# Seven products for eight in half of the up projections, with the sums of weights on GpSimd

## The chip, the core and the metric

The kernel runs on one core of a Trainium2 chip. The metric is the device time of one execution in microseconds (us). Engines: PE (TensorE, matrix products), PEld (its weight loads), DVE (VectorE), ACT (ScalarE), POOL (GpSimd), SP (the queue that issues the weight loads). Each engine works through its own queue in order; semaphores hold an instruction until what it reads is there and what it overwrites is free.

## The reference, cut to what matters

One decoder layer on 256 tokens, width 2048, everything float32: a feed-forward, a token-mixing block, a second feed-forward, a layer norm behind each.

```python
def swiglu(x, w_up, w_down):                 # w_up [2048, 2 * 5632], w_down [5632, 2048]
    a, u = jnp.split(x @ w_up, 2, axis=-1)
    return (jax.nn.silu(a) * u) @ w_down

h = layer_norm(ALPHA * h + 0.5 * swiglu(h, w_ffn1_up, w_ffn1_down), ln1_g, ln1_b)
h = layer_norm(ALPHA * h + token_mix(h, ...), ln2_g, ln2_b)
h = layer_norm(ALPHA * h + 0.5 * swiglu(h, w_ffn2_up, w_ffn2_down), ln3_g, ln3_b)
```

## The kernel before, in words

**Precision.** PE multiplies in float32r, so that each float32 operand is split into a high and a low part, h + l (`split`): ACT copies and rounds the source to h (L92), DVE subtracts h from the source to get l (L93). A product is three matmuls: ah·wh, ah·wl, al·wh.

**A product of activations and weights** is `gemm`. Activations lie feature-major in pages of 128 x 1024 (four k tiles of 128 rows by 256 tokens). Weights come in groups of 512 rows by 512 columns, 1 MB each, which SP loads into one of three `raw` buffers; each group is split in two halves of 128 x 1024 into `wh` and `wl`, four buffers each. A half serves 12 matmuls (2 k tiles, 2 token tiles of 128, 3 matmuls). The two sums of 128 tokens by 512 columns are PSUM banks `acc`.

**The feed-forward** (`ffn`) goes over 11 chunks j of 512 hidden columns. Chunk j is two gemms of 4 groups over the same activations: columns j of the half a, and columns NFF + j of the half u, 192 matmuls together. Then ACT takes tanh and DVE makes silu(a) * u (L206 to L208) in `tmp`; PE transposes it in 8 transposes (L166), which are put behind a group of the next chunk (`later`, `tick`), and the result is split into the next pages. After all 11 chunks `project_norm` does the down projection in 4 gemms of 11 groups, adds the residual (L235) and does the layer norm; the reciprocal root in it is the only arithmetic of POOL (L245, one column).

**Order.** The kernel is written in a framework that puts the instructions into each engine's queue by priority and by its own costs; what stands in the queues is fixed when the program is built.

Of the kernel before, what the change touches and what calls it, by code (L numbers as in the profile page):

```python
# [36 lines left out]
GL0 = 10  # L37


class Layer:  # L40
# [58 lines left out]
    def raw(self, shape=(P, 4, 512)):  # L99
        return self.tile("raw", list(shape), F32, 3)  # L100

    def load_w(self, src, paged=False, cut=None):
# [4 lines left out]
        out = []
        for i in range(2):
            if cut is not None:
                cut(i)  # L110
                self.nc.sync.dma_start(raw[:, 2 * i:2 * i + 2, :], src[:, 2 * i:2 * i + 2, :])
            if paged:
                h, l = (self.page(F32R).rearrange("p (k n) -> p k n", k=2) for _ in range(2))
            else:
                h = self.tile("wh", [P, 2, 512], F32R, 4)
                l = self.tile("wl", [P, 2, 512], F32R, 4)
            self.split(h, l, raw[:, 2 * i:2 * i + 2, :])
            out.append((h, l))
# [69 lines left out]
    def ffn(self, xh, xl, w_up, w_down, resid, g, b, finish, before_last=None, before=None, cut=None,  # L188
# [3 lines left out]
        hh, hl = [], []  # L192

        def place(ts, ph, pl):
            for tt in range(2):
# [1 line left out]
            yield

        for j in range(NFF):
            a = self.gemm(act, w_up[j], 4, head=4 if j == 0 and before is None else 0, before=before if j == 0 else None,  # L200
                          cut=cut if j == 0 else None)
            u = self.gemm(act, w_up[NFF + j], 4)
            ph, pl = self.page(F32R), self.page(F32R)
            ts = [self.tmp(), self.tmp()]
            for tt, t in enumerate(ts):
                nc.scalar.activation(t, a[tt], AF.Tanh, scale=0.5)  # L206
                nc.vector.scalar_tensor_tensor(t, t, 1.0, a[tt], op0=ALU.add, op1=ALU.mult)  # L207
                nc.vector.scalar_tensor_tensor(t, t, 0.25, u[tt], op0=ALU.mult, op1=ALU.mult)  # L208
# [481 lines left out]
```

## Time and profile before

| | |
|---|---|
| median of three timed runs | 2240.55 us (2240.1 to 2241.12) |
| span of the profiled execution, from its first to its last instruction | 2238.4 us |
| PE, share of the span in which it is busy | 99% |
| DVE | 56% |
| ACT | 43% |
| POOL | 2% |
| granted TensorE clock, mean | 0.998 |
| mean transfer rate | 198 GB/s |

The three runs and the profiled span agree within 0.13%. The profile lists, for each engine, when each instruction ran, and what ended the idle time before it; the granted clock is the share of TensorE's full speed.

### The profile page before, as it was taken

The numbers are of one execution on the slowest core, as the hardware profiler recorded it, in microseconds if no ns is written. First come the engines' busy times: TensorE is split into PE (matmuls) and PEld (weight loads), VectorE is DVE, ScalarE is ACT, GpSimd is POOL, SyncE is SP. The second block draws the span as 40 slices with busy tenths as digits, with TensorE's granted clock in tenths as the row PEclk, the third lists the DMA queues.
The fourth block names the chain that finished last, engine by engine and source line by source line (L and its number), as shares of the span: only waits on it lengthen the run. The fifth ranks groups of instructions, "written<-read, shape, count | busy, mean of one in ns | idle before, by whom it ended". The sixth has DMA issues, their size and how long they took to land.

```text
span 2238.4 us, 24924 instructions
## 1 busy us (share of the span) xinstructions
PE 2215.9 (99%) x10056; PEld 1838.5 (82%) x10056; DVE 1248.9 (56%) x1404; ACT 958.2 (43%) x1075; POOL 51.2 (2%) x93
## 2 busy tenths in 40 slices
PE   8999999999999999999999999999999999999997
PEld 6888888888888888888888888878888888888886
DVE  5555555554455757675566556675555555454445
ACT  4444444443334444554444444444444444443332
POOL 0000000010000100000000000010000000000000
PEclk9999999999999999999999999999999999999999
DMA  7555555565556645455655556666555555565553
GB/s 261 191 188 188 188 188 188 189 253 205 199 188 228 233 170 182 169 184 188 207 179 194 199 193 220 235 221 239 188 188 188 189 190 191 188 211 197 188 192 128
DMA packets 65956, 442.34 MB, mean 198 GB/s; under 512 B 7905, under 2 KB 7905, under 8 KB 15537
## 3 DMA queue, kind: packets, MB, share of 16 engines
q1 hardware_dynamic: 57888, 414.21, 52.4%
q0 software_dynamic: 6656, 22.36, 3.4%
q10 hardware_dynamic: 1296, 4.19, 0.5%
q8 instruction: 78, 1.28, 0.2%
q14 instruction: 38, 0.30, 0.0%
HBM read 434.44 MB, written 6.29 MB: 197 GB/s over the span
## 4 chain that ended last, share of the span: by engine, by line
PE 96%; DVE 2%; DMA 1%; issue 0%; ACT 0%; POOL 0%; POOLq 0%; ACTq 0%; DVEq 0%
PE acc L133 93%; PE tr L166 2%; PE tr L282 1%; DMA pg<-in_xT 1%; DVE wl L93 0%; DVE pg L562 0%; DMA tmp<-in_w_pool 0%; DVE gt L252 0%; DVE m L561 0%; PE tr L314 0%; DVE pg L93 0%; DVE gt L254 0%; DVE stats L236 0%; DVE gt L235 0%; POOL mv L245 0%
## 5 line engine op out<-in xcount | busy, mean ns | idle before, releaser
L133 PE MATMUL acc<-wh,pg 128*128 128x512 f32 x5120 | 1594.2, 390 | 0.0
L93 DVE TENSOR_TENSOR wl<-raw,wh 128x1024 fp32r<-128x1024 f32 x772 | 944.4, 1224 | 917.2 <-ACT wh L92 916.7
L92 ACT CAST wh<-raw 128x1024 fp32r<-128x1024 f32 x772 | 812.7, 1054 | 1130.6 <-PE acc L133 1099.2
L133 PEld LDWEIGHTS acc<-wh,pg 128*128 128x128 f32 x5120 | 961.2, 188 | 198.3
L133 PE MATMUL acc<-wl,pg 128*128 128x512 f32 x2560 | 996.4, 389 | 0.0
L133 PEld LDWEIGHTS acc<-wl,pg 128*128 128x128 f32 x2560 | 480.7, 188 | 98.0
L133 PE MATMUL acc<-wh,gt 128*128 128x512 f32 x1056 | 332.8, 391 | 7.8 <-ACT wh L92 7.2
L133 PEld LDWEIGHTS acc<-wh,gt 128*128 128x128 f32 x1056 | 198.9, 189 | 49.3 <-ACT wh L92 7.2
L133 PE MATMUL acc<-wl,gt 128*128 128x512 f32 x528 | 206.4, 391 | 1.0 <-DVE wl L93 1.0
L133 PEld LDWEIGHTS acc<-wl,gt 128*128 128x128 f32 x528 | 99.6, 189 | 22.2 <-DVE wl L93 1.8
L92 ACT CAST pg<-tr 128x512 fp32r<-128x512 f32 x82 | 44.7, 586 | 20.4 <-PE tr L166 19.8
L93 DVE TENSOR_TENSOR pg<-tr,pg 128x512 fp32r<-128x512 f32 x82 | 52.5, 682 | 0.6 <-ACT pg L92 0.3
L206 ACT ACTIVATE tmp<-acc 128x512 f32<-128x512 f32 x44 | 26.2, 595 | 26.0 <-PE acc L133 26.0
L207 DVE SCALAR_TENSOR_TENSOR tmp<-tmp,acc 128x512 f32<-128x512 f32 x44 | 30.1, 684 | 10.3 <-ACT tmp L206 10.3
L133 PE MATMUL acc<-pg,pg 128*128 128x512 f32 x144 | 34.5, 392 | 0.8 <-DVE pg L93 0.7
L133 PEld LDWEIGHTS acc<-pg,pg 128*128 128x128 f32 x144 | 26.8, 188 | 7.1 <-DVE pg L93 1.6
L166 PEld LDWEIGHTS tr<-ident,tmp 128*128 128x128 f32 x240 | 27.9, 140 | 3.9
L166 PE MATMUL tr<-ident,tmp 128*128 128x128 f32 x240 | 31.0, 272 | 0.0
L208 DVE SCALAR_TENSOR_TENSOR tmp<-tmp,acc 128x512 f32<-128x512 f32 x44 | 28.1, 680 | 0.0
L235 DVE SCALAR_TENSOR_TENSOR gt<-gt,acc 128x512 f32<-128x512 f32 x24 | 15.7, 682 | 21.5 <-PE acc L133 21.5
L282 PE MATMUL tr<-pg,pg 128*128 128x256 f32 (+2 forms) x168 | 26.3, 302 | 0.0
L93 DVE TENSOR_TENSOR pg<-raw,pg 128x1024 fp32r<-128x1024 f32 x18 | 21.7, 1217 | 4.5 <-ACT pg L92 4.5
(99 smaller groups left out, 418.4 us busy)
## 6 DMA issues: line engine op xcount, KB each, us to landing
raw<-in_up SPq DMA_DIRECT2D x175, 1024.0 KB, 4.8
raw<-in_down SPq DMA_DIRECT2D x88, 1024.0 KB, 4.8
raw<-in_w_in SPq DMA_DIRECT2D x88, 1024.0 KB, 4.8
raw<-in_w_out SPq DMA_DIRECT2D x16, 1024.0 KB, 5.1
raw<-in_w_kv SPq DMA_DIRECT2D x8, 1024.0 KB, 5.0
raw<-in_br_att SPq DMA_DIRECT2D x8, 1024.0 KB, 4.8
h_d<-gt POOLq DMA_DIRECT2D x16, 256.0 KB, 3.6
raw<-in_br_pool SPq DMA_DIRECT2D x4, 1024.0 KB, 4.8
```

Source lines behind the costliest of these rows:

```text
L92: self.nc.scalar.copy(h, src)
L93: self.nc.vector.tensor_sub(l, src, h.bitcast(F32))
L133: nc.tensor.matmul(accs[tt], lhsT=a, rhs=b, start=kt == 0 and i == 0, stop=kt == kts - 1 and i == 2)
L166: self.nc.tensor.transpose(t[:, i * P:(i + 1) * P], src[:, i * P:(i + 1) * P], self.ident)
L206: nc.scalar.activation(t, a[tt], AF.Tanh, scale=0.5)
L207: nc.vector.scalar_tensor_tensor(t, t, 1.0, a[tt], op0=ALU.add, op1=ALU.mult)
L208: nc.vector.scalar_tensor_tensor(t, t, 0.25, u[tt], op0=ALU.mult, op1=ALU.mult)
L235: nc.vector.scalar_tensor_tensor(zz, zz, ALPHA, accs[tt], op0=ALU.mult, op1=ALU.add)
L282: self.nc.tensor.matmul(out, lhsT=a, rhs=b, start=start and i == 0, stop=stop and i == 2)
```

## The change

Both feed-forwards are changed; the token mixing keeps its order of work.

**Seven for eight.** In a chunk j > 0 the groups of k, 512 rows each, are treated jointly for both token tiles, both halves of k and both column blocks (a and u): a 2 x 2 by 2 x 2 block product, eight block products of 6 matmuls each. In two of the four groups (`SEVEN`) they are done in the Strassen-Winograd manner as seven: one is between sums of the activations (`forms`, made once for each feed-forward) and sums of weight quarters. The weight quarters b00, b10, b01, b11 are halves of 128 x 1024. Four sums of them are made by POOL in place: two (below called A and B) at the head of a group, C and D one after the other later. Each of the seven multiplies its own split operand, so that a group of seven splits 7 halves in place of 4, and each split half serves 6 matmuls. The other two groups stay at eight products, but take their token difference from `forms`. At the end of a chunk eight instructions combine seven PSUM banks to the four results.

**Columns in three parts.** The 11 chunks come as 4, 4 and 3 (`HIDDEN`); behind each part comes its share of the down projection, which is added to the residual in SBUF (`Norm.add`).

**Buffers.** `raw` is 9 halves in place of 3 whole groups, and every load is 512 KB in place of 1 MB; pages 23 in place of 27, `tmp` 6 in place of 4; PSUM is one pool of 8 banks in place of 4 and 4. x's pages come from the pool `pg`; memory pages are loaded in the first two groups of the last gemm of the first feed-forward.

```diff
+PAGES = dict(pg=23, gt=6)
+HIDDEN = ((0, 4), (4, 8), (8, NFF))
+SEVEN = (True, True, False, False)
...
-    def raw(self, shape=(P, 4, 512)):
-        return self.tile("raw", list(shape), F32, 3)
+    def raw(self, shape=(P, 2, 512)):
+        return self.tile("raw", list(shape), F32, 9)
+
+    def load_half(self, src, i):
+        raw = self.raw()
+        self.nc.sync.dma_start(raw, src[:, 2 * i:2 * i + 2, :])
+        return raw
...
+    def seven(self, act, forms, modes, w0, w1):
...
+        def product(g, bank, lhs, w, last):
...
+            for k in range(2):
+                ah, al = lhs(k)
+                for i, (a, b) in enumerate(((ah, w[0]), (ah, w[1]), (al, w[0]))):
+                    nc.tensor.matmul(banks[bank], lhsT=a, rhs=b[:, k, :], start=bank not in first,
+                                     stop=last and k == 1 and i == 2)
...
+        def singles(g, end):
+
+            b00, b10 = self.load_half(w0[g], 0), self.load_half(w0[g], 1)
+            b11 = self.load_half(w1[g], 1)
+            b01 = self.load_half(w1[g], 0)
+            s00 = self.halves(b00)
+            nc.gpsimd.tensor_add(b00, b00, b01)
+            nc.gpsimd.tensor_add(b01, b01, b11)
+            product(g, 1, quarter(g, 0, 0), s00, g == sevens[-1])
+            s10 = self.halves(b10)
+            product(g, 2, quarter(g, 0, 1), s10, end)
+            s11 = self.halves(b11)
+            product(g, 3, form(g, 3), s11, end)
+
+            def sums():
+                t1 = self.halves(b00)
+                nc.gpsimd.tensor_add(b00, b00, b11)
+                product(g, 5, form(g, 0), t1, end)
+                t2 = self.halves(b00)
+                nc.gpsimd.tensor_add(b00, b00, b10)
+                product(g, 6, form(g, 1), t2, g == sevens[-1])
+                t3 = self.halves(b01)
+                product(g, 7, form(g, 2), t3, g == sevens[-1])
+                t4 = self.halves(b00)
+                product(g, 4, quarter(g, 1, 1), t4, end)
+
+            return sums
...
+        for g in range(groups):
+            end = g == groups - 1
+            if modes[g]:
+                after = singles(g, end)
+            else:
+                eight(g, end)
+                after = None
+            if behind is not None:
+                behind()
+            behind = after
+            self.tick()
...
+        u, c00, v, c11 = (self.tmp() for _ in range(4))
+        nc.scalar.copy(u, banks[1])
+        nc.vector.tensor_add(c00, u, banks[2])
+        nc.vector.tensor_add(u, u, banks[6])
+        nc.vector.tensor_add(v, u, banks[7])
+        nc.vector.tensor_sub(u, banks[5], u)
+        nc.vector.tensor_sub(c11, banks[5], v)
+        nc.vector.tensor_add(u, u, banks[3])
+        nc.vector.tensor_add(v, v, banks[4])
+        return [[c00, u], [v, c11]]
```

The order of a chunk is thus: three single quarters of group 0, three of group 1, the four sums t1 to t4 of group 0, the four quarters of group 2 (eight products), t1 to t4 of group 1, the four quarters of group 3.

DVE's queue at the border of two chunks before: `tmp` is the chunk that ended, `wl` are halves of the next one.

```order
L93 TENSOR_TENSOR wl_1039<-raw_1036,wh_1038 128x1024
L208 SCALAR_TENSOR_TENSOR tmp_978<-tmp_978,acc_838 128x512
L208 SCALAR_TENSOR_TENSOR tmp_979<-tmp_979,acc_839 128x512
L93 TENSOR_TENSOR wl_1043<-raw_1036,wh_1042 128x1024
L93 TENSOR_TENSOR wl_1073<-raw_1070,wh_1072 128x1024
```

DVE's queue in the changed kernel, behind the last matmul of a chunk (the first row needs it): the end of that chunk, the three singles of the next chunk's group 1 (`wl_1198`, `wl_1210`, `wl_1220`).

```order
L287 TENSOR_TENSOR tmp_1117<-acc_883,tmp_1117 128x512
L288 TENSOR_TENSOR tmp_1120<-acc_883,tmp_1119 128x512
L289 TENSOR_TENSOR tmp_1117<-tmp_1117,acc_824 128x512
L290 TENSOR_TENSOR tmp_1119<-tmp_1119,acc_917 128x512
L352 SCALAR_TENSOR_TENSOR tmp_1131<-tmp_1131,tmp_1118 128x512
L96 TENSOR_TENSOR wl_1198<-raw_1189,wh_1197 128x1024
L353 SCALAR_TENSOR_TENSOR tmp_1131<-tmp_1131,tmp_1117 128x512
L352 SCALAR_TENSOR_TENSOR tmp_1132<-tmp_1132,tmp_1119 128x512
L96 TENSOR_TENSOR wl_1210<-raw_1191,wh_1209 128x1024
L353 SCALAR_TENSOR_TENSOR tmp_1132<-tmp_1132,tmp_1120 128x512
L96 TENSOR_TENSOR pg_1130<-tr_1182,pg_1129 128x4x128
L96 TENSOR_TENSOR wl_1220<-raw_1193,wh_1219 128x1024
```

Two instructions of the chunk that ended stood between two halves; now ten do (of its eight combinations four, the four of silu, a transposed split), and they stand among the splits of three halves.

The next rows of DVE's queue are t1, t2, t3, t4 of group 0 and the first quarter of group 2; with what each waits for.

```order
L96 TENSOR_TENSOR wl_1230<-raw_1139,wh_1229 128x1024 [waits Pool_49]
L96 TENSOR_TENSOR wl_1242<-raw_1139,wh_1241 128x1024 [waits PE_49,Activation_49]
L96 TENSOR_TENSOR wl_1254<-raw_1145,wh_1253 128x1024 [waits Activation_49]
L96 TENSOR_TENSOR wl_1265<-raw_1139,wh_1264 128x1024 [waits Activation_49]
L96 TENSOR_TENSOR wl_1291<-raw_1282,wh_1290 128x1024 [waits DMAHW5_49,Activation_49]
```

POOL's queue in that chunk: A and B of group 0 (`raw_1139` is its b00), A and B of group 1 (`raw_1189`), C and D of group 0, C and D of group 1.

```order
L231 TENSOR_TENSOR raw_1139<-raw_1139,raw_1145 128x1024 [waits DMAHW5_49,DMAHW0_49,DVE_49]
L232 TENSOR_TENSOR raw_1145<-raw_1145,raw_1143 128x1024 [waits DMAHW7_49,Pool_49]
L231 TENSOR_TENSOR raw_1189<-raw_1189,raw_1195 128x1024 [waits DMAHW1_49,DMAHW4_49,DVE_49,Activation_49]
L232 TENSOR_TENSOR raw_1195<-raw_1195,raw_1193 128x1024 [waits DMAHW6_49,DMAHW3_49,Pool_49]
L241 TENSOR_TENSOR raw_1139<-raw_1139,raw_1143 128x1024 [waits DVE_49,Activation_49]
L244 TENSOR_TENSOR raw_1139<-raw_1139,raw_1141 128x1024 [waits DMAHW6_49,DVE_49]
L241 TENSOR_TENSOR raw_1189<-raw_1189,raw_1193 128x1024 [waits DVE_49]
L244 TENSOR_TENSOR raw_1189<-raw_1189,raw_1191 128x1024 [waits DMAHW2_49,DVE_49]
```

Before, none of these eight stood there. C overwrites b00, which t1's split reads, so it stands behind that subtraction; t2's copy on ACT reads what C wrote; D overwrites b00 again behind t2's subtraction, and t4's copy reads what D wrote.

PE's queue there: the products of t2 (`wh_1241`), t3 (`wh_1253`) and t4 (`wh_1264`), then group 2 (`wh_1290`).

```order
L215 MATMUL acc_1246<-wh_1241,pg_252 128x512 [waits Activation_49]
L215 MATMUL acc_1257<-wh_1253,pg_252 128x512 [waits Activation_49]
L215 MATMUL acc_1246<-wl_1242,pg_252 128x512 [waits DVE_49]
...
L215 MATMUL acc_1268<-wh_1264,pg_71 128x512 [waits Activation_49]
...
L215 MATMUL acc_1164<-wh_1290,pg_73 128x512 [waits Activation_49]
L215 MATMUL acc_1268<-wl_1265,pg_71 128x512 [waits DVE_49]
```

Of the chunk's 188 PE instructions (180 matmuls and 8 transposes) 64 stand ahead of that last row, the 8 transposes among them, and 124 matmuls from it on.

## Rows read from the trace of the kernel before

**Rows 1.** The page: span, then busy us of each engine, its share, instructions.
```profile
span 2238.4 us, 24924 instructions
PE 2215.9 (99%) x10056; PEld 1838.5 (82%) x10056; DVE 1248.9 (56%) x1404; ACT 958.2 (43%) x1075; POOL 51.2 (2%) x93
```

**Rows 2.** Stretches: us, PE, PEld, DVE, ACT, POOL busy (x), PEclk, DMA share, GB/s.
```profile
40.00:515.00 475.00, 475.00 (x2142) 394.26 (x2141) 248.74 (x236) 201.92 (x213) 8.50 (x16) 1.00 0.56 197
560.00:765.00 205.00, 205.00 (x916) 169.90 (x915) 117.58 (x123) 86.20 (x86) 8.00 (x11) 1.00 0.60 211
1300.00:1510.00 210.00, 208.39 (x939) 171.43 (x939) 134.61 (x156) 88.06 (x95) 17.25 (x31) 1.00 0.62 218
```

**Rows 3.** Chain that ended last, in order of time: start us, us, what.
```profile
61.46 43.54 PE acc L133 x192
105.88 43.54 PE acc L133 x192
```

**Rows 4.** The page's groups: line engine op out<-in | busy, mean ns | idle before.
```profile
L93 DVE TENSOR_TENSOR wl<-raw,wh 128x1024 fp32r<-128x1024 f32 x772 | 944.4, 1224 | 917.2 <-ACT wh L92 916.7
L92 ACT CAST wh<-raw 128x1024 fp32r<-128x1024 f32 x772 | 812.7, 1054 | 1130.6 <-PE acc L133 1099.2
```

**Rows 5.** Timeline inside a chunk: start us, us, engine, line, [idle before <-releaser].
```profile
305.34 1.05 ACT L92 CAST wh<-raw 128x1024 fp32r<-128x1024 f32 x1 [1.67 <-PE acc L133]
...
306.43 1.22 DVE L93 TENSOR_TENSOR wl<-raw,wh 128x1024 fp32r<-128x1024 f32 x1 [1.49 <-ACT wh L92]
```

**Rows 6.** Timeline of DVE in a stretch without idle time.
```profile
1493.32 1.22 DVE L93 TENSOR_TENSOR pg<-raw,pg 128x1024 fp32r<-128x1024 f32 x1
1494.45 1.22 DVE L93 TENSOR_TENSOR wl<-raw,wh 128x1024 fp32r<-128x1024 f32 x1
1495.59 0.68 DVE L235 SCALAR_TENSOR_TENSOR gt<-gt,acc 128x512 f32<-128x512 f32 x1
1496.19 1.22 DVE L93 TENSOR_TENSOR pg<-raw,pg 128x1024 fp32r<-128x1024 f32 x1
```

**Rows 7.** POOL's arithmetic, all six: duration ns min/median/max.
```profile
L245 POOL TENSOR_TENSOR mv<-mv,mhalf x6: 922/932/2101, 736.2 to 2229.0; 128x1 f32<-128x1 f32 x6
```

**Rows 8.** Timelines of POOL and of DVE around the first of them.
```profile
736.18 0.93 POOL L245 TENSOR_TENSOR mv<-mv,mhalf 128x1 f32<-128x1 f32 x1 [238.52 <-DVE mv L244]
...
735.95 0.74 DVE L252 SCALAR_TENSOR_TENSOR gt<-gt,mv,gt 128x512 f32<-128x512 f32 x1
737.14 0.22 DVE L246 SCALAR_TENSOR_TENSOR mv<-mv 128x1 f32<-128x1 f32 x1 [0.46 <-POOL mv L245]
```

**Rows 9.** Timelines of POOL and of DVE around the longest of them.
```profile
752.23 2.10 POOL L245 TENSOR_TENSOR mv<-mv,mhalf 128x1 f32<-128x1 f32 x1
...
751.36 1.41 DVE L252 SCALAR_TENSOR_TENSOR gt<-gt,mv,gt 128x512 f32<-128x512 f32 x2
752.68 1.22 DVE L93 TENSOR_TENSOR wl<-raw,wh 128x1024 fp32r<-128x1024 f32 x1
754.37 0.22 DVE L246 SCALAR_TENSOR_TENSOR mv<-mv 128x1 f32<-128x1 f32 x1 [0.47 <-POOL mv L245]
```

**Rows 10.** The page's DMA issues: KB each, median us from issue to landing.
```profile
raw<-in_up SPq DMA_DIRECT2D x175, 1024.0 KB, 4.8
```

**Rows 11.** Timeline of DVE at the end: first and last of one token half's norm.
```profile
2216.07 0.69 DVE L235 SCALAR_TENSOR_TENSOR gt<-gt,acc 128x512 f32<-128x512 f32 x1 [8.57 <-PE acc L133]
...
2222.66 1.41 DVE L254 SCALAR_TENSOR_TENSOR gt<-gt,mv,pg 128x512 f32<-128x512 f32 x2
```

More of the change, by code (lines that the diff above doesn't have):

```diff
@@ L110, in load_w @@
                 cut(i)
[L111 to L118, printed above, removed]
+            out.append(self.halves(self.load_half(src, i), paged))
         return out
@@ L153, in gemm, with forms @@
         return accs
+    def forms(self, hp, lp, modes):
+        nc = self.nc
+        out = []
+        for g, seven in enumerate(modes):
+            a = self.page()
+            nc.vector.tensor_add(a, hp[g].bitcast(F32), lp[g].bitcast(F32))
+            if seven:
+                q = a.rearrange("p (j k i t) -> p i j k t", j=2, k=2, i=2)
+                f = self.page()
+                fv = f.rearrange("p (f k t) -> p f k t", f=4, k=2)
+                nc.vector.tensor_sub(fv[:, 0], q[:, 1, 0], q[:, 1, 1])
+                nc.vector.tensor_sub(fv[:, 1], fv[:, 0], q[:, 0, 0])
+                nc.vector.tensor_sub(fv[:, 2], q[:, 0, 0], q[:, 1, 0])
+                nc.vector.tensor_add(fv[:, 3], q[:, 0, 1], fv[:, 1])
+                h, l = self.page(F32R), self.page(F32R)
+                self.split(h, l, f)
+            else:
+                q = a.rearrange("p (k i t) -> p i k t", k=4, i=2)
+                f = self.tmp()
+                nc.vector.tensor_sub(f.rearrange("p (k t) -> p k t", k=4), q[:, 0], q[:, 1])
+                both = self.page(F32R)
+                h, l = both[:, :512], both[:, 512:]
+                self.split(h, l, f)
+            out.append((h, l))
+        return out
@@ L196, in place @@
                 self.to_feature(ts[tt], ph, pl, tt)
[L197 to L208, printed above, removed]
-            self.later(place(ts, ph, pl))
-            hh.append(ph)
-            hl.append(pl)
@@ new lines, in place @@
+                yield
+        for lo, hi in HIDDEN:
+            hh, hl = [], []
+            for j in range(lo, hi):
+                if j == 0:
+                    a = self.gemm(act, w_up[0], 4, head=4 if before is None else 0, before=before, cut=cut)
+                    forms = self.forms(xh, xl, SEVEN)
+                    u = self.gemm(act, w_up[NFF], 4)
+                else:
+                    c = self.seven(act, forms, SEVEN, w_up[j], w_up[NFF + j])
+                    a, u = ([c[tt][i] for tt in range(2)] for i in range(2))
+                ph, pl = self.page(F32R), self.page(F32R)
+                ts = [self.tmp(), self.tmp()]
+                for tt, t in enumerate(ts):
+                    nc.scalar.activation(t, a[tt], AF.Tanh, scale=0.5)
+                    nc.vector.scalar_tensor_tensor(t, t, 1.0, a[tt], op0=ALU.add, op1=ALU.mult)
+                    nc.vector.scalar_tensor_tensor(t, t, 0.25, u[tt], op0=ALU.mult, op1=ALU.mult)
+                self.later(place(ts, ph, pl))
+                hh.append(ph)
+                hl.append(pl)
+            last = hi == NFF
+            if lo == 0:
+                norm.load()
+            if last:
+                norm.load_scales()
+            w = [w_down[n][lo:hi] for n in range(ND)]
+            norm.add(self.act_pages(hh, hl), w, hi - lo, lo == 0, last, before_last,
+                     3 if before_last is None else 2)
@@ L258, in norm_to_feature, with project_norm @@
+        norm.finish(finish, filler)
+    def project_norm(self, act, w, groups, resid, g, b, finish):
+        norm = Norm(self, resid, g, b)
+        norm.load()
+        norm.load_scales()
+        norm.add(act, w, groups, True, True, None, 4)
+        norm.finish(finish)
     def norm_to_feature(self, dram):
@@ L361, in layer_kernel @@
     h2_d = L.dram.tile([SEQ, D_MODEL], F32, name="h2_d")
-    xh = L.pages(ND, tags=("gt",) * 3)
-    xl = L.pages(ND, tags=("gt",) * 3)
+    xh = L.pages(ND)
+    xl = L.pages(ND)
     mem = ([], [])
     def load_mem(g):
-        if g in (4, 6, 8, 10):
+        for _ in range(2 if g < 2 else 0):
             for p in mem:
```

165 lines of the change are left out of this document (107 added, 58 removed).

## The prediction

> **What bounds the kernel now.** I read the page's first part, then stretches, then the chain that ended last, then timelines. PE is busy for 2215.9 of 2238.4 us [rows 1], in both kinds of feed-forward stretch for all of it, at clock 1.00 [rows 2]. In the chain a chunk of 192 matmuls is one piece of 43.54 us, and the next begins 105.88 - 61.46 = 44.42 us later [rows 3]: a matmul costs 43.54 / 192 = 0.2268 us, the 8 transposes between them 0.88. ACT and DVE wait for PE all the time (1099 and 917 us of idle time, [rows 4]): what they prepare is ready early, limited by the four `wh` and `wl` buffers. So a matmul less is worth 0.2268 us as long as ACT, DVE and now POOL stay ahead. Whether they do is a question of the order in one chunk, not of their shares.
>
> **What is removed.** A group of seven has 42 matmuls for 48; two groups, ten chunks, two feed-forwards: 240 matmuls, 54.4 us. If PE never waited, a chunk would last 41.7 us and the kernel 2240.55 - 54.4 = 2186.
>
> **What is added in sum.** A chunk now has 22 splits for 16. Back to back on DVE a split costs 1.14 us and a 512-column instruction 0.60 (1494.45 to 1495.59 to 1496.19, [rows 6]). 22 splits and 13 small ones (seven combinations, four of silu, two transposed splits) are 25.1 + 7.8 = 32.9 us of 41.7. ACT's 22 copies at 1.054 [rows 4] are 23.2. Both fit; the sums don't decide.
>
> **The path of a chunk.** Time 0 is the last matmul of the chunk before. PE has three halves in stock, 18 matmuls or 4.1 us. DVE's queue holds nine small instructions and the splits of group 1's three singles and of t1, in order: 9 x 0.60 + 4 x 1.14 = 10.0, so t1's subtraction ends at about 10.1. PE has by then done its 36 single matmuls and 4 transposes (8.6) and waits. From here each sum is a link: POOL's add may start only when the subtraction has read b00, ACT's copy when the add has ended, DVE's subtraction behind that, and DVE's queue holds nothing else to do between t1 and t2. A copy of 1.05 and a subtraction of 1.22 follow each other within 0.05 [rows 5]; with P for the add, a link is P + 2.42. C's link puts t2 at 12.5 + P. t3 needs no late sum and follows 1.14 later; D's link puts t4 at 14.9 + 2P. 124 matmuls stand behind that in PE's queue, 28.1 us. A chunk lasts 43.0 + 2P. In group 1 the same two links come under group 2's 48 matmuls: t1 is split 7.4 after group 0's t4 (five splits, one small, about 1.1 for a load into a buffer that D frees; landing took 4.8 for 1 MB, [rows 10]), t4 12.2 + 2P after it, and PE wants that after 71 matmuls, 16.1: a wait of 2P - 3.9 where positive.
>
> Six of the 20 chunks (j = 1, 4, 8) follow no chunk of the new kind, so the crowd at their head is small. There t1's copy waits for a `wh` buffer, free after 18 matmuls, and t1 is split at 4.1 + 2.3 = 6.4 in place of 10.1. With the transposes, which now fall into the down part, such a chunk costs 40.2 + 2P and the same wait.
>
> **The cost of an add.** No row has a 128x1024 add on POOL. Its only arithmetic has one column and takes 0.93 us, once 2.10 [rows 7]; in the first of them 0.42 of it lie behind the end of a DVE instruction (736.69 to 737.11, [rows 8]), so the fixed cost I take is 0.42. Columns cost DVE (1.14 - 0.60) / 512 = 1.05 ns each. Lower bound 0.42 + 1.08 = 1.5; upper, if POOL takes the two operands one after the other, 0.42 + 2.16 = 2.6. No row is nearer to one end: P = 2.05. The Trainium skill (GPSIMD Engine Reference, Elementwise — side-by-side cycle accounting) gives 4497 ns for 2048 columns; half of it, an estimate, is 2.25 and would make my sum below 2437.
>
> **The adds against DVE's queue.** Rows 7 to 9 show more. In the longest case DVE ran L252 and then a split without a gap; both read two operands from SBUF. POOL's instruction began at 752.23, before the split (752.68), and yet ended at 754.33, 0.43 behind the split's end (753.90) [rows 9]; in the first case it ended 0.42 behind DVE's [rows 8]. I read this as: an instruction of POOL that reads SBUF is held while DVE runs instructions with two SBUF operands, and a DVE queue without gaps goes first. The Trainium skill (SBUF — State Buffer, Who interferes with whom) has such a pair exclude each other for a whole instruction, first come first served. The trace agrees with the exclusion and not with the order of service; by that order A and B would each stop DVE for a whole add, 4.1 for the 3.5 below, and the sum would be 8 us higher.
>
> What the hold costs: (a) A and B of group 1 stand in POOL's queue ahead of C, and DVE's crowd has one instruction, the transposed split, without two SBUF operands; so A and B run mainly while DVE waits for C: 2P - 0.6 = 3.5. In a light chunk 2P. (b) D becomes startable when t3's subtraction begins, and is held for it: 1.1. (c) The same for D of group 1: 1.1 more of wait, 2P - 2.8 = 1.3 together. (d) A and B of the next group 0 run in the last 6 us of a chunk, where DVE has two splits of its own: DVE comes P - 1.2 = 0.85 late to the border.
>
> **The sum.** Full chunk: 43.0 + 4.1 + 3.5 + 1.1 + 1.3 + 0.85 = 53.85, 9.4 more than 44.42. Light chunk: 40.2 + 4.1 + 4.1 + 1.1 + 1.3 = 50.8, 6.4 more. 14 x 9.4 + 6 x 6.4 = 170 us. On the profiled span of 2238.4 that is 2408, on the median 2240.55, which is 0.1% above it, **2411**.
>
> **Costed at nothing.** `forms`: per feed-forward four adds of pages, eight of 256 columns, two splits of a page and four half-size instructions, some 12 us of DVE beside 8 splits (9.1) under a gemm of 96 matmuls, 21.8 us, with up to 8 us of halves in stock; uncovered, 2 or 3 us each. The 16 further residual adds of a feed-forward, 10 us of DVE, lie in down projections, where DVE was busy 118 of 205 us [rows 2]. Twice as many loads of half the size: the DMA share is 0.56 to 0.62 [rows 2]. Four pages less and one PSUM pool: PE's order in the token mixing is unchanged and it idled 1.6 us in its last stretch [rows 2]; up to 5. The end: the last gemm now holds 3 groups, 36 matmuls or 8.2 us behind which the norm of the first token half must be over; it takes 2216.07 to 2224.07, 8.0 [rows 11].
>
> **Rivals.** *No hold*: POOL reads beside DVE at will, and the long case of [rows 9] had another reason. Then a full chunk is 43.0 + 4.1 + 0.2 = 47.3, a light one 44.5: +41, 2282; with P from 1.5 to 2.6, 2256 to 2326. For it: no DVE split in the trace was ever longer than 1.227. Against it: [rows 8, 9]. *The saving comes through*: adds so short that the links vanish under PE's work. Without a hold the break-even is where 14 x (43.0 + 2P - 44.42) + 6 x (40.2 + 2P - 44.42) = 0, P = 1.13; at the fixed 0.42 alone the two terms give -28, 2212, and no case can pass 2186. The lower bound of 1.5 speaks against it; for it, that POOL's time per column is in no row. *The change moves nothing*, P near 1.1: within 0.2% of before, which is about what a measurement of this kernel can tell from none.
>
> **Chances.** The hold as summed 0.67: with P from 1.5 (full 50.0, light 47.5, +97) to 2.6 (57.7 and 54.1, +244), 2338 to 2485. No hold, slower 0.20. The saving 0.09. Nothing 0.04. The range 2280 to 2480 leaves out the two last and the lower third of no hold. Faster by over 0.2%: 0.09; within: 0.04; slower: 0.87.
>
> **What would show it.** Right: DVE idle between t1's and t2's split for 3.5 us and more, released by ACT, which was released by POOL; chunks of about 54 us, the first of a part shorter; POOL's adds longer where DVE's splits run beside them, the second pair of a chunk late; PE waiting for `wl` and `wh` in the first 25 us of a chunk and not in groups 2 and 3. Wrong: adds below 1.2 us, or PE without waits at t2 and t4. A granted clock below 1.00 in the chunks would add to the time; nothing of it is in the sum, since no stretch with idle PE shows it [rows 2].

## The result and the profile after

The changed kernel takes 2467.68 us (median of four runs, 2464.3 to 2471.08), the kernel before 2240.84 in the same session: ratio 1.1013, 95% interval 1.1 to 1.1026. That is 226.8 us slower, where 2411 (2280 to 2480) was forecast. The profiled span went from 2238.4 to 2469.3 us.

The page of the changed kernel, the lines of [rows 1] and two lines of 40 slices (busy tenths of PE, and PE's granted clock):

```profile
span 2469.3 us, 26390 instructions
...
PE 2272.1 (92%) x9816; PEld 1827.1 (74%) x9816; DVE 1624.9 (66%) x1732; ACT 1083.3 (44%) x1223; POOL 506.9 (21%) x254
...
PE   7889998799988999999999999989799888998798
...
PEclk9999999999999999999999999999899999999999
```

240 matmuls are gone from PE's list, and yet PE is busy longer, and idle for 197 us where it was for 22. The slices in the middle, the token mixing, are full as before; the loss is in the two feed-forwards. I read it by chunks, each from the first of the two L353 instructions that end one (L208 before) to that of the next (start times in DVE's timeline), against 44.42 before; the losses add up to 230.5 of the 230.9 us by which the span grew:

| stretch | us lost |
|---|---|
| 14 full chunks, mean 55.64 | +157 |
| 4 light chunks (j = 4, 8), 52.97 after 87.09 for the down part's 384 matmuls | +34 |
| 2 light chunks j = 1, 51.5 and 51.8 from the first chunk's L353 to the first combination (L287) behind their own last matmul | +14.5 |
| first chunk of the first feed-forward, 66.69 for 54.69 | +12 |
| from the first feed-forward's last chunk to the second's first | +13 |
| behind the last chunk | 0 |

POOL's sums, by line (columns as in [rows 4]; L231 and L232 are the two first sums of a group, A and B; L241 and L244 the later ones, C and D):

```profile
L244 POOL TENSOR_TENSOR raw<-raw,raw 128x1024 f32<-128x1024 f32 x40 | 131.9, 3297 | 96.7 <-DVE wl L96 96.7
L232 POOL TENSOR_TENSOR raw<-raw,raw 128x1024 f32<-128x1024 f32 x40 | 121.6, 3039 | 3.1
L231 POOL TENSOR_TENSOR raw<-raw,raw 128x1024 f32<-128x1024 f32 x40 | 106.2, 2655 | 682.5 <-DMA raw<-in_up 387.9 <-DVE wl L96 219.8 <-ACT wh L95 74.8
L241 POOL TENSOR_TENSOR raw<-raw,raw 128x1024 f32<-128x1024 f32 x40 | 95.4, 2386 | 257.5 <-DVE wl L96 239.6 <-DMA raw<-in_up 17.9
```

C always runs while DVE waits for it: its 2.39 us are P, the undisturbed price of a sum. D, with a split of DVE beside it, takes 3.30. DVE's side of the same thing, where [rows 4] had 1224 ns for a split:

```profile
L96 DVE TENSOR_TENSOR wl<-raw,wh 128x1024 fp32r<-128x1024 f32 x894 | 1170.3, 1328 | 779.5 <-ACT wh L95 773.6 <-DMA raw<-in_w_in 2.9 <-DMA raw<-in_w_kv 1.5
L352 DVE SCALAR_TENSOR_TENSOR tmp<-tmp,tmp 128x512 f32<-128x512 f32 x40 | 57.7, 1443 | 0.0
...
L353 DVE SCALAR_TENSOR_TENSOR tmp<-tmp,tmp 128x512 f32<-128x512 f32 x40 | 27.2, 679 | 0.0
```

L352 and L353 are the same kind of instruction of the same size; L352 has twice the mean, because in each of the 14 full chunks one of its two takes 2.85 to 2.87, with A beside it; all others take 0.68 or 0.69. The waits of the changed kernel (engine, line, waited for, us, times, longest) name the chain:

```profile
ACT wh L95 <- POOL raw L241: 263.2, 40, 10.1
POOL raw L241 <- DVE wl L96: 239.6, 38, 10.3
...
ACT wh L95 <- POOL raw L244: 148.7, 40, 3.7
...
PE acc L215 <- DVE wl L96: 101.0, 69, 4.5
POOL raw L244 <- DVE wl L96: 96.7, 40, 2.4
```

One full chunk, j = 3 of the first feed-forward, in the timeline of all engines. The last matmul before it began at 173.23 and ended at 173.62:

```profile
170.37 3.27 POOL L232 TENSOR_TENSOR raw<-raw,raw 128x1024 f32<-128x1024 f32 x1
...
172.02 2.69 DVE L96 TENSOR_TENSOR wl<-raw,wh 128x1024 fp32r<-128x1024 f32 x1 [0.65 <-ACT wh L95]
...
174.64 0.68 DVE L287 TENSOR_TENSOR tmp<-acc,tmp 128x512 f32<-128x512 f32 x1
...
178.77 0.68 DVE L353 SCALAR_TENSOR_TENSOR tmp<-tmp,tmp 128x512 f32<-128x512 f32 x1
...
178.98 2.70 POOL L231 TENSOR_TENSOR raw<-raw,raw 128x1024 f32<-128x1024 f32 x1 [5.34 <-ACT wh L95]
179.37 2.86 DVE L352 SCALAR_TENSOR_TENSOR tmp<-tmp,tmp 128x512 f32<-128x512 f32 x1
...
181.76 2.67 POOL L232 TENSOR_TENSOR raw<-raw,raw 128x1024 f32<-128x1024 f32 x1
182.16 3.35 DVE L96 TENSOR_TENSOR wl<-raw,wh 128x1024 fp32r<-128x1024 f32 x1
...
185.56 0.50 PE L215 MATMUL acc<-wl,pg 128*128 128x512 f32 x1 [4.47 <-DVE wl L96]
...
186.63 2.34 DVE L96 TENSOR_TENSOR wl<-raw,wh 128x1024 fp32r<-128x1024 f32 x2
...
189.12 2.37 POOL L241 TENSOR_TENSOR raw<-raw,raw 128x1024 f32<-128x1024 f32 x1 [4.70 <-DVE wl L96]
...
191.52 1.99 ACT L95 CAST wh<-raw 128x1024 fp32r<-128x1024 f32 x2 [10.04 <-POOL raw L241]
192.60 2.36 DVE L96 TENSOR_TENSOR wl<-raw,wh 128x1024 fp32r<-128x1024 f32 x2 [3.62 <-ACT wh L95]
...
193.91 3.29 POOL L244 TENSOR_TENSOR raw<-raw,raw 128x1024 f32<-128x1024 f32 x1 [2.42 <-DVE wl L96]
197.23 2.95 ACT L95 CAST wh<-raw 128x1024 fp32r<-128x1024 f32 x3 [3.71 <-POOL raw L244]
198.30 3.50 DVE L96 TENSOR_TENSOR wl<-raw,wh 128x1024 fp32r<-128x1024 f32 x3 [3.34 <-ACT wh L95]
198.32 0.50 PE L215 MATMUL acc<-wh,pg 128*128 128x512 f32 x1 [1.88 <-ACT wh L95]
```

The first half shows the **hold**: POOL and DVE take turns. L287 needs only the last matmul, but stands behind a split that takes 2.69 beside B of the next chunk's group 0, and begins 1.0 late. A begins in L353 and takes 0.3 more than P; L352 begins in A and ends 0.55 behind it; B runs, the split of 1.22 takes 3.35 and ends 1.1 behind B, and PE has waited 4.47 for it. The second half shows the **links**: C starts 0.15 behind t1's split, ACT 0.03 behind C, DVE 0.03 behind ACT's first copy: t1's split ends at 186.63 + 2.34 = 188.97 and t2's at 192.60 + 1.22 = 193.82, 4.85 later; for t4, with D held, it is 5.70. The same chunk in stretches (columns as in [rows 2]):

```profile
180.00:185.00 5.00, 1.09 (x6) 0.57 (x4) 5.00 (x2) 1.17 (x2) 4.35 (x2) 1.00 0.00 0
185.00:190.00 5.00, 3.88 (x10) 2.66 (x11) 3.98 (x5) 0.00 (x0) 0.88 (x1) 0.64 0.01 3
190.00:195.00 5.00, 4.76 (x13) 2.77 (x12) 2.36 (x2) 1.99 (x2) 2.58 (x2) 0.67 0.30 107
...
200.00:205.00 5.00, 5.00 (x17) 3.93 (x16) 4.66 (x5) 2.74 (x4) 0.00 (x0) 0.66 1.00 392
205.00:230.39 25.39, 24.91 (x110) 20.32 (x109) 14.90 (x15) 11.11 (x12) 5.70 (x2) 1.00 0.72 253
```

DVE is busy for the whole of 180 to 185 with two instructions. From 205 on, through groups 2 and 3, PE has one wait left, for one of group 1's sums:

```profile
218.04 0.50 PE L215 MATMUL acc<-wl,pg 128*128 128x512 f32 x1 [0.48 <-DVE wl L96]
```

The chunk is typical in its first half: in all 14 full chunks L287 begins 1.0 us behind the last matmul's end, t1's split ends 14.3 behind L287's start, t2's 4.86 later and t4's 5.71 behind that.

### The profile page after: what moved, and what is told of

It is laid out like the page before. It is cut to its first block, busy times and chain, and to the rows that moved or that the text cites. A ratio compares the mean times of both kernels' runs of the same rounds, so it can differ in the third digit from the quotient of the medians.

```text
span 2469.3 us, 26390 instructions
## 1 busy us (share of the span) xinstructions
PE 2272.1 (92%) x9816; PEld 1827.1 (74%) x9816; DVE 1624.9 (66%) x1732; ACT 1083.3 (44%) x1223; POOL 506.9 (21%) x254
## 4 chain that ended last, share of the span: by engine, by line
PE 46%; issue 9%; POOL 7%; DVE 6%; ACT 2%; DMA 1%; POOLq 0%; DVEq 0%; ACTq 0%
PE acc L141 39%; PE acc L215 5%; POOL raw L244 3%; DVE wl L96 3%; ACT wh L95 2%; POOL raw L241 2%; PE tr L399 1%; DVE tmp L352 1%; PE tr L304 1%; DMA raw<-in_up 1%; POOL raw L231 1%; POOL raw L232 1%; DVE tmp L353 0%; DVE pg L96 0%; DVE tmp L287 0%
## 5 line engine op out<-in xcount | busy, mean ns | idle before, releaser
L96 DVE TENSOR_TENSOR wl<-raw,wh 128x1024 fp32r<-128x1024 f32 x894 | 1170.3, 1328 | 779.5 <-ACT wh L95 773.6
L95 ACT CAST wh<-raw 128x1024 fp32r<-128x1024 f32 x894 | 924.1, 1051 | 1230.8 <-PE acc L141 586.8
L141 PE MATMUL acc<-wh,pg 128*128 128x512 f32 x3632 | 1138.3, 392 | 13.1 <-ACT wh L95 7.5
L215 PE MATMUL acc<-wh,pg 128*128 128x512 f32 x2400 | 803.5, 411 | 58.2 <-ACT wh L95 57.8
L141 PEld LDWEIGHTS acc<-wh,pg 128*128 128x128 f32 x3632 | 683.8, 188 | 157.0 <-ACT wh L95 7.5
L141 PE MATMUL acc<-wl,pg 128*128 128x512 f32 x1816 | 708.9, 390 | 0.6 <-DVE wl L96 0.6
L215 PEld LDWEIGHTS acc<-wh,pg 128*128 128x128 f32 x2400 | 476.6, 199 | 178.4 <-ACT wh L95 83.1
L215 PE MATMUL acc<-wl,pg 128*128 128x512 f32 x1200 | 505.0, 421 | 101.1 <-DVE wl L96 101.0
L141 PEld LDWEIGHTS acc<-wl,pg 128*128 128x128 f32 x1816 | 342.1, 188 | 71.1 <-DVE wl L96 1.3
L215 PEld LDWEIGHTS acc<-wl,pg 128*128 128x128 f32 x1200 | 239.4, 200 | 191.1 <-DVE wl L96 139.8
L231 POOL TENSOR_TENSOR raw<-raw,raw 128x1024 f32<-128x1024 f32 x40 | 106.2, 2655 | 682.5 <-DMA raw<-in_up 387.9
L244 POOL TENSOR_TENSOR raw<-raw,raw 128x1024 f32<-128x1024 f32 x40 | 131.9, 3297 | 96.7 <-DVE wl L96 96.7
L241 POOL TENSOR_TENSOR raw<-raw,raw 128x1024 f32<-128x1024 f32 x40 | 95.4, 2386 | 257.5 <-DVE wl L96 239.6
L232 POOL TENSOR_TENSOR raw<-raw,raw 128x1024 f32<-128x1024 f32 x40 | 121.6, 3039 | 3.1
L352 DVE SCALAR_TENSOR_TENSOR tmp<-tmp,tmp 128x512 f32<-128x512 f32 x40 | 57.7, 1443 | 0.0
L516 POOL TENSOR_TENSOR mv<-mv,mhalf 128x1 f32<-128x1 f32 x6 | 7.0, 1160 | 241.4 <-DVE mv L515 241.4
L477 POOL DMA_DIRECT2D gt<-h_d x16 | 8.5, 537 | 212.6 <-DVE gt L777 204.7
```

Of the source, the lines that this page charges most:

```text
L95: self.nc.scalar.copy(h, src)
L96: self.nc.vector.tensor_sub(l, src, h.bitcast(F32))
L141: nc.tensor.matmul(accs[tt], lhsT=a, rhs=b, start=kt == 0 and i == 0, stop=kt == kts - 1 and i == 2)
L215: nc.tensor.matmul(banks[bank], lhsT=a, rhs=b[:, k, :], start=bank not in first, stop=last and k == 1 and i == 2)
L231: nc.gpsimd.tensor_add(b00, b00, b01)
L232: nc.gpsimd.tensor_add(b01, b01, b11)
```

## The experiments

Two theories: the **hold** (POOL's reads keep DVE from its two-operand instructions), and the **links** (sum, copy and subtraction in a chain, whoever computes the sum). A third candidate are the parts of the change that have nothing to do with seven products.

| run | us | ratio to before, 95% interval | full chunk |
|---|---|---|---|
| before | 2240.84 | | 44.42 |
| after | 2467.68 | 1.1013 (1.1 to 1.1026) | 55.64 |
| e1 parts alone | 2262.54 | 1.0094 (1.0077 to 1.0111) | 44.47 |
| e2 no sums | 2230.93 | 0.9955 (0.9939 to 0.9971) | 43.34 |
| e3 sums unread | 2454.74 | 1.0954 (1.0932 to 1.0976) | 48 to 58 |
| e4 memsets | 2231.46 | 0.9956 (0.994 to 0.9972) | 43.33 |
| e5 links, no reads | 2331.43 | 1.0406 (1.039 to 1.0421) | 48.6 to 49.5 |
| e6 sums on VectorE | 2341.05 | 1.0448 (1.0432 to 1.0463) | 49.1 to 49.5 |
| e7 parts mended | 2243.17 | 1.0013 (1.0003 to 1.0023) | 44.47 |
| e8 sevens apart | 2426.5 | 1.083 (1.0814 to 1.0847) | 51 to 55 |
| e9 apart, freed, VectorE | 2234.25 | 0.9973 (0.9962 to 0.9984) | 44.03 |
| e10 one seven of that | 2235.59 | 0.9979 (0.997 to 0.9988) | 43.55 |
| e11 e9 on GpSimd | 2427.62 | 1.0838 (1.0822 to 1.0855) | 53.5 to 54.7 |
| e12 e9, ends mended | 2224.47 | 0.9934 (0.992 to 0.9947) | 44.03 |

**e1, the parts alone.**

```diff
-                    forms = self.forms(xh, xl, SEVEN)
...
-                    c = self.seven(act, forms, SEVEN, w_up[j], w_up[NFF + j])
...
+                u = self.gemm(act, w_up[NFF + j], 4)
```

> The columns in three parts, the half-size loads and the new buffers alone: every chunk is two plain products as before, without forms, sevens or GpSimd sums. My theory (the loss lies in the dependent GpSimd sums and in GpSimd and VectorE excluding each other): 2238 to 2250 us, chunks of 44.4 us. Rival (the parts, the loads or fewer pages cost much of the 227 us): 2280 us or more.

It took 2262.54: missed, 21.7 us that I had put at nothing, with chunks of 44.47. They lie in two places. The first chunk ends (first L353 or L208, as above) at 64.36 where it ended at 54.69: POOL's timeline shows the residual rows (8 x 256 KB) and then four loads of norm weights sent off in the first 16 us, beside the first input pages,

```profile
2.51 3.17 POOL L473 DMA_DIRECT2D gt<-in_x  x6
7.51 1.06 POOL L473 DMA_DIRECT2D gt<-in_x  x2 [1.83 <-DMA ident<-in_consts]
```

because the `gt` pages that they fill no longer hold x. And from the first feed-forward's last chunk to the second's first it takes 881.4 us, 12.4 more than before (1043.2, less 174.2 for the 768 matmuls of the down projection that now lie elsewhere); there PE's timeline has one wait,

```profile
1517.95 3.57 PE L304 MATMUL tr<-ident,gt 128*128 128x128 f32 x16 [9.45 <-DVE gt L521]
```

in front of the second token tile's transposes. In the kernel before, PE's order has the first tile's 24 held products ahead of the last of these transposes: its trace has the 24 from 1495.00 to 1501.98 and those transposes from 1504.71 on. In e1 and in the changed kernel all 24 stand behind them.

**e2, no sums**: the four `gpsimd.tensor_add` lines left out.

> The four sums of weight quarters of each group are left out, and their splits read the quarters as loaded, so the result is not the reference's; all else stays, seven products, 22 splits, eight combinations. My theory: the links t1 to t2 to t4 vanish, PE is kept, 42 to 44 us for a full chunk, and the kernel takes 2200 to 2235 us (2186 and what the forms cost in the first chunks, 10 to 20 us). Rival (VectorE's crowd of splits and combinations, or the clock, is the loss, and the sums matter little): 2350 us or more, full chunks over 50 us.

2230.93, inside. The surprise is how little 240 matmuls bring even when sums are free. The light chunks last 128.79 - 87.09 = 41.70, the full saving. The others last 43.34, 1.64 more:

```profile
1852.95:1896.32 43.37, 42.35 (x190) 34.41 (x189) 34.02 (x36) 25.59 (x28) 0.00 (x0) 1.00 0.57 194
```

DVE's combinations and silu of one chunk stand ahead of the first splits of the next, and a group of seven gives only six matmuls a split to hide behind.

**e3, the sums unread**: the same four sums, written to scratch.

```diff
-            nc.gpsimd.tensor_add(b00, b00, b01)
+            nc.gpsimd.tensor_add(self.tile("sc", [P, 2, 512], mybir.dt.bfloat16), b00, b01)
```

> GpSimd does the four adds with the same inputs, but writes them to a scratch buffer (in bfloat16) that nobody reads; the splits read the quarters as loaded, so the result is not the reference's. No split waits for an add any more, only the port is shared. My theory (GpSimd's reads and VectorE's instructions with two SBUF operands exclude each other): VectorE's 22 splits and 4 two-operand instructions (27.5 us) and eight adds of 2.39 (19.1) add up to 46.6 us, so a full chunk takes 46 to 52 us, VectorE's longest splits are near 3.5 us, and the kernel takes 2290 to 2390 us. Rival (no exclusion, the links are all of it): as the run without adds within 10 us.

2454.74, above my range: no split waits for a sum, and nearly the whole loss is there, 223.8 us over e2. The timeline at a chunk's border shows which instructions of DVE are held:

```profile
2020.29 3.27 POOL L241 TENSOR_TENSOR sc<-raw,raw 128x1024 bf16<-128x1024 f32 x1
2021.22 0.68 DVE L287 TENSOR_TENSOR tmp<-acc,tmp 128x512 f32<-128x512 f32 x1
...
2023.02 0.67 DVE L290 TENSOR_TENSOR tmp<-tmp,acc 128x512 f32<-128x512 f32 x1
...
2023.65 2.85 POOL L244 TENSOR_TENSOR sc<-raw,raw 128x1024 bf16<-128x1024 f32 x1
...
2024.22 3.37 DVE L96 TENSOR_TENSOR wl<-raw,wh 128x1024 fp32r<-128x1024 f32 x1
...
2027.51 2.84 DVE L353 SCALAR_TENSOR_TENSOR tmp<-tmp,tmp 128x512 f32<-128x512 f32 x1
```

L287 to L290, which take one operand from PSUM (`acc`), run at 0.68 in the middle of a sum. The split and L353, both operands from SBUF, last 2.15 and 2.16 us longer, nearly a whole sum. It goes on so:

```profile
2026.58 3.21 POOL L241 TENSOR_TENSOR sc<-raw,raw 128x1024 bf16<-128x1024 f32 x1
...
2029.87 2.70 POOL L244 TENSOR_TENSOR sc<-raw,raw 128x1024 bf16<-128x1024 f32 x1
2030.27 2.85 DVE L352 SCALAR_TENSOR_TENSOR tmp<-tmp,tmp 128x512 f32<-128x512 f32 x1
...
2035.38 9.16 DVE L96 TENSOR_TENSOR wl<-raw,wh 128x1024 fp32r<-128x1024 f32 x8
```

Nothing keeps C and D away from the border here, and all four stand in DVE's crowd: t1's split, the second of the last row's eight, ends at 2037.7, 18.3 us behind the end of the last matmul (2019.4). In e2 that is 10.1 in every full chunk, in the changed kernel 15.4.

**e4, memsets** of as many columns in the place of the sums.

> The four adds are replaced by GpSimd memsets of as many columns to a scratch buffer (bfloat16) that nobody reads; the splits read the quarters as loaded, so the result is not the reference's. My theory (it is GpSimd's reading that excludes VectorE): as the run without adds within 10 us, no split over 1.3 us. Rival (any GpSimd instruction that is in SBUF holds VectorE): splits lengthened and 15 us or more above the run without adds.

2231.46, as e2: POOL's writing costs DVE nothing, so e3's loss is its reading. A memset is shorter than a sum (0.96 us), but e5 below writes for as long as the sums ran, and DVE's splits have a mean of 1222 ns in both, as in e2.

**e5, the links without reads**: memsets of the sum's own tile, 2.39 us in all, where each sum stood.

```diff
-                nc.gpsimd.tensor_add(b00, b00, b11)
+                nc.gpsimd.memset(b00, 0.0)
+                nc.gpsimd.memset(b00, 0.0)
+                nc.gpsimd.memset(b00[:, :1], 0.0)
```

> Each sum is replaced by three memsets of the tile that the sum wrote (two whole, one half: 2.39 us by the 0.955 us that a memset took in e4, as long as an undisturbed sum), so that the sums' values are left out but every wait stays: the split of t1 before the third, that before the split of t2, that before the fourth, that before the split of t4. GpSimd reads nothing. If the links between the splits cost what the prediction gave them (full chunk 43.0 + 2P and 2P - 3.9 for the second group, light chunk 40.2 + 2P, no hold), P = 2.39 gives 48.7 and 45.0 us a chunk against the 43.34 of e2, and 2231 + 14 x 5.4 + 6 x 1.7 = 2317: 2285 to 2340. If the hold of VectorE by GpSimd's reads is the whole loss, the time stays within 10 us of e2's 2231.

2331.43, inside my range and 100 us above e4. Eleven of the 14 full chunks last 48.6, three 49.3 to 49.5:

```profile
1927.68:1976.26 48.58, 45.02 (x190) 35.20 (x189) 33.62 (x37) 24.75 (x28) 19.39 (x24) 0.96 0.51 173
```

The prediction's path without its hold gives 43.0 + 2P + 2P - 3.9 = 48.66 at P = 2.39. For the light chunks (I left the second wait out of their 45.0) it gives 40.2 + 4P - 3.9 = 45.86; the first of each feed-forward's two took 132.99 - 87.09 = 45.90, the second 47.5. The trace bears out the two links at the head: in the full chunks t1's split ends 10.1 behind the last matmul and t4's 9.95 later, for 10.1 and 9.6 in the prediction. It doesn't bear out the second wait (2P - 3.9, 0.9 us): PE has none behind group 2, and needs 28.6 us or more behind t4's split for the 28.1 of the sum. So the links were worked out rightly, and the agreement to a tenth is in part luck. From here to the changed kernel the hold costs another 136.2 us, 6.8 a chunk.

**e6, the sums on VectorE**: `gpsimd` becomes `vector` in the four lines.

> The four sums run on VectorE, the rest is as changed. Eight more instructions of about 1.22 us make 9.8 us a chunk: VectorE has 34.0 busy us in the 43.34 us chunk of e2, so 43.8 with them. Hold theory: no engine is held any more, VectorE becomes about as busy as TensorE, the chunk takes 45 to 48 us: 2265 to 2325, over 130 us faster than the changed kernel. Rival (the chain of sum and split is the price, whichever engine adds): 2400 or more.

2341.05, 16 us above my range and 126.6 us faster than the changed kernel. DVE's own sums cost about as much as e5's links: in its order t1's split now stands behind the first two sums of the second group too, and t2's and t4's behind C and D.

**e7, the parts mended**: e1 with residual loads behind a one-column POOL copy of the first chunk's `tmp`, and with PSUM pools of four and four.

> Run e1 (three parts, half loads, pages; all chunks plain) with two edits: the residual rows are loaded only after the first chunk (behind a small GpSimd copy of that chunk's last column), and transposes and sums have PSUM buffers of their own again, four each. If e1's 21.7 us are the 3.1 MB of residual and norm loads that now run beside the first input pages (first chunk 9.7 us later) and TensorE's 9.4 us wait for the second token tile at the second feed-forward's start, the time returns to 2238 to 2247. If the half loads or the pages cost the time, it stays at 2255 or more.

2243.17, inside: the first chunk ends at 57.28, and the step between the feed-forwards takes 868.2, 0.8 less than before. Half loads, pages and parts cost 2 or 3 us together.

**e8, the sevens apart.**

```diff
-SEVEN = (True, True, False, False)
+SEVEN = (True, False, True, False)
```

> Same work as changed, with the groups of seven in places 1 and 3 instead of 1 and 2, each followed by a group of eight, so that only one group's sums stand at the chunk's border. Undisturbed sums take 8 x 2.39 = 19.1 us a chunk and VectorE's own 34.0 us, of which some 7 us read PSUM and are not held: 46 to 47 us at the least if the rest excludes the sums. Theory (a hold costs where VectorE has no slack, at the border): chunk 47 to 51, 2305 to 2390. Rival (VectorE and the sums are one resource that is full all through the chunk, wherever the sums stand): 2430 or more.

2426.5: 41 us better than the changed kernel, but 36 us above my range and nearer the rival. In the waits PE no longer stands still for 4 us at a border but a little everywhere:

```profile
PE acc L218 <- DVE wl L96: 153.3, 123, 2.3
```

**e9, apart, with freed quarters, on VectorE.** Each group of seven is done whole behind a group of eight, no sum waits for the split of another sum, and the residual loads are held back as in e7. A further edit, not shown, makes two PSUM tiles ahead of the norm and was meant to put PE's order at the second border right:

```diff
-SEVEN = (True, True, False, False)
+SEVEN = (False, True, False, True)
...
             product(g, 3, form(g, 3), s11, end)
+            nc.vector.tensor_add(b01, b01, b11)
+            nc.vector.tensor_add(b11, b00, b11)
...
                 t1 = self.halves(b00)
-                nc.gpsimd.tensor_add(b00, b00, b11)
+                nc.vector.tensor_add(b10, b11, b10)
...
-                t2 = self.halves(b00)
-                nc.gpsimd.tensor_add(b00, b00, b10)
+                t2 = self.halves(b11)
...
-                t4 = self.halves(b00)
+                t4 = self.halves(b10)
```

> The sums on VectorE as in e6, but the groups of seven in places 2 and 4, each done whole behind a group of eight; the third sum goes into b11 and the fourth into b10, whose own splits are done by then, so no sum waits for the split of another sum; and the loads and the second border mended as in e7. VectorE needs 34.0 + 9.8 = 43.8 us a chunk, TensorE 180 x 0.2268 + 0.87 = 41.7. If the links made e6's 49.5 us, the chunk now takes 43.8 to 46, and the time is 2231 - 19 + 20 x (0.5 to 2.7): 2222 to 2266. If VectorE's load alone made them, the chunk stays at 48 to 50 and the time at 2300 or more.

2234.25, inside: faster than the kernel before by 0.27%. The further edit did nothing: PE's wait at the second border is still there, 9.5 us, and so it is in e10 and e11, which have the same edit (9.4 and 9.5). The window of one chunk:

```profile
1899.83:1943.86 44.03, 42.63 (x190) 34.39 (x188) 42.58 (x44) 25.39 (x28) 0.00 (x0) 1.00 0.54 192
```

DVE is busy for 42.58 of 44.03: it has become the second wall, which fits that two groups of seven gain no more than one (e10, where it is busy for 35.0 of 43.55).

**e10, one seven** in the same arrangement (place 2).

> As e9, with one group of seven in a chunk (place 2): 186 matmuls, 42.2 us, and 0.87 us of transposes make 43.1; VectorE has 34.0 - 3 x 1.2 + 4.9 = 35.3. If the 1.6 us by which e2's chunk was longer than its matmuls is VectorE's crowd at the chunk's border in front of a group of seven, a group of eight there hides it: 43.1 to 43.9 a chunk, 2243 - 20 x (0.5 to 1.4) + 3 for the forms: 2216 to 2236, faster than both kernels. If that crowd costs the same before any group: 2245 or more.

2235.59, at the upper end. The chunk of 43.55 is 0.5 above its 186 matmuls and 8 transposes (43.06): a group of eight at the border hides nearly all of what cost e2 1.64.

**e11, e9 with its sums on GpSimd.** Only the engine of the four sums differs.

> As e9, with the four sums on GpSimd: no links, sums away from the border, values right; only the engine of the sums differs. If the hold needs no link and no crowd to cost, VectorE's 34.0 us and the sums' 19 to 24 us share the chunk, of which 7 us of VectorE's are not held: 46 to 53 us, 2265 to 2420. If the loss came from the links and the border, GpSimd takes the sums off VectorE: within 15 us of e9 or faster.

2427.62, 8 us above my range: 193.4 us for the engine alone, though no sum waits for another's split and a group of eight stands at each border. This is the hold and the longer sum together, for t1 to t4 still wait for their sums; that the hold needs no such wait is e3's result. The same stretch as e9's:

```profile
1997.26:2051.68 54.42, 47.16 (x179) 36.39 (x178) 39.54 (x37) 24.11 (x26) 24.42 (x8) 0.84 0.44 154
```

GpSimd took 9.8 us of sums off DVE's queue and DVE's busy time fell by 3; the eight sums last 24.42, not 8 x 2.39 = 19.1.

**e12, e9 with both ends mended**: the second token tile's transposes go into the first's four PSUM tiles, which puts PE's order back to that of before (e9's edit for this is left out), and the forms are built one group behind each group of the second product of the first chunk.

```diff
-                    forms = self.forms(xh, xl, SEVEN)
+                    forms = []
+                    self.later(self.forms(xh, xl, SEVEN, forms))
...
+            trs = [self.tr() for _ in range(ND)]
...
-                self.to_feature(zz, hp[n], lp[n], tt)
+                self.to_feature(zz, hp[n], lp[n], tt, t=trs[n])
```

> As e9, with two edits: the second token tile's transposes at the norm go into the same four PSUM tiles as the first's (so that TensorE's order has the first tile's 24 held products ahead of them again, as in the kernel before), and the forms are built one group behind each group of the second product of the first chunk instead of all ahead of it. The wait of 9.4 us at the second feed-forward's start goes if the order made it, and of the first chunks' 4.5 us that e9 still loses in each half some 2 to 4 us: 2234 - 9 - 2 x (0 to 4) = 2217 to 2226. If the 9.4 us are the norm itself and not the order, the time stays at 2230 or more.

2224.47, inside, and 0.66% faster than the kernel before (0.992 to 0.9947). The wait of 9.5 us is gone (the longest that is left there is 0.4); the forms brought nothing that shows (the first step within each feed-forward is 48.58 where e9 had 48.55 and 48.62).

```profile
span 2222.4 us, 26387 instructions
...
PE 2177.0 (98%) x9816; PEld 1789.9 (81%) x9816; DVE 1678.8 (76%) x1892; ACT 1096.3 (49%) x1223; POOL 52.0 (2%) x96
```

## Why the prediction was right in kind and short by 57 us

**What bounds.** Right: a matmul is worth 0.2268 us where nothing else ends later. e2's light chunks gain the full 2.72, and its full ones show that DVE's order at the border, not DVE's share, takes 1.64 of it back.

**The path.** Right at the head of a chunk, link by link: 4.85 from t1's split to t2's for P + 2.42 = 4.81, and in e5 10.07 to t1's split for 10.1. The wait behind group 2 was not there in e5. "No hold", the rival at 2282, is e5: with P = 2.39 its terms make 14 x 4.24 + 6 x 1.44 = 68, and with e1's 22 us 2331, which is what e5 took, to within the luck told there. What excluded that rival is the hold, not the links.

**The hold.** Right in place and nearly in size, wrong in its order of service. By terms, in all full chunks: (d) L287 begins 1.0 late, for 0.85. (a) t1's split ends 14.3 behind L287's start where e5 and e2 have 10.0: 4.3 for 3.5. (b) D is 0.9 longer, for 1.1. (c) One wait of 0.5 to 0.7 behind group 2, for 1.3. "A DVE queue without gaps goes first" fails: at the border the split, L352 and the next split each waited for the sum that had begun before them. That (a) comes out near all the same is luck: whether A and B fall behind the crowd or the crowd waits for A and B, two sums stand in the path. The Trainium skill (SBUF — State Buffer, Who interferes with whom) has such a pair exclude each other in order of issue, and counts only GpSimd's instructions that read SBUF and only VectorE's with two SBUF inputs. The traces agree: the exclusion and the order in L352's 2.86 us for 0.68, the reads in e3's 223.8 us against e4's 0.5 over e2, the two operands in e3's 0.68 for L287 to L290 against 2.84 for L353. What held the long POOL instruction of [rows 9] past a DVE instruction that began after it stays open.

**The mis-sized term: P.** The step "No row is nearer to one end: P = 2.05" gave 2.05 for a sum that takes 2.39. It enters a full chunk seven times (39.5 + 7P) and a light one six times (38.5 + 6P). At 2.39 these are 56.2 and 52.8. From last matmul to last matmul a full chunk took 56.06 (the table's marks give 55.64, because six of the 14 end before a down part, where L287 is not late), the light ones 52.0 and, at j = 1, 50.6. The sum becomes 2240.55 + 216 = 2456, with e1's 22 us 2478, and 8 of the 10 us that this is above the measured time are the light chunks. So P and the parts make up the miss. The Trainium skill's figure (GPSIMD Engine Reference, Elementwise — side-by-side cycle accounting) gave an estimate of 2.25, nearer than mine; the rows decide for 2.39.

**What was put at nothing.** "Four pages less and one PSUM pool ... up to 5" is the step that failed: e1 shows 21.7 us of loads moved to the start and of PE's order at the second border, e7 and e12 that these two are the cause. "A granted clock below 1.00 ... nothing of it is in the sum": the stretches at 0.64 to 0.67 are in the measured chunk; from 200 to 205 PE was busy throughout and began 17 matmuls, 22 at 0.2268, so 1.1 us there. Behind t4's split, where PE is the path, matmuls spaced wider than 0.2268 so cost 1.2 to 1.9 us in 8 of the 14 full chunks, all with a clock below 1.00 there, and 0.3 in the other six, as in e5. That a full chunk still comes out at 56.06 for 56.2 is luck again: at P = 2.39 (c) is 2.0, and most of what its wait fell short of that went to the clock.

**How the loss divides.** Taking the pieces away in the order of the runs: matmuls -54.4, the crowd at 14 borders +23 (e2), the parts +22 (e1), the links +100 (e5 over e4), the hold +136 (after over e5): +227. The two last don't add: the hold without links costs 224 (e3 over e2), and the links on top of it 13. The traces show why: without links C and D come to the border too, and t1's split ends 18.3 us and more behind the last matmul, but t4's follows 3.4 to 5.6 later; with links it ends 15.4 behind, and t4's follows 10.6 later. The chain that delays C and D also keeps them out of DVE's crowd. Moving the sums away from the border, which I had expected to save 80 us or more, saved 41 (e8).

## What to carry to other kernels

Before work goes to GpSimd because it is idle, look at what its instructions read and at what VectorE runs meanwhile: a sum of two SBUF operands there cost 193 us more than the same sum on a VectorE that was already busy for 34 of 43 us a chunk. Write a derived value into a buffer whose reader is done, not over one that is about to be read, and put the stage with the most vector work a matmul behind one with little; e9 did both and held the residual loads back, and no run divides its 107 us under e6 among the three. And time the rearrangement that makes room for a change by itself: here it cost 22 us in two places far from the change, and both were mended.

## What the runs showed of the hardware that I had not expected

- A 128x1024 float32 sum on GpSimd: 2.39 us alone, 3.30 with a split of VectorE in it; a memset of the same columns 0.96. On VectorE the sum took 1.22.
- The held instruction of VectorE waits until the sum that began before it has ended, and the two engines then alternate: splits of 3.35 and 3.37 for 1.22, half-size instructions of 2.86 for 0.68.
- The granted clock: 0.64 to 0.67 over 5 us in stretches behind waits of 1.9 to 4.5 us, so partly at the lower level of 1.2 GHz, and 1.00 again in the second half of the chunk. In e11's chunk shown it was 0.84, with waits of 1.2 to 2 us; in e9's, where the longest wait is 0.86, it was 1.00.
